# Keeping B's product operands in DRAM and splitting two of seven products once more in a two-level Strassen matmul with GELU

Groups, products and steps are counted from one in the prose, as in the prediction (the code counts from zero).

## Chip, cores, metric

One core of one Trainium2 chip. The metric is the device time of one launch in microseconds, measured as the median of several runs of the same kernel. Runs before the change agree within 0.2%. All runs in this document are fast: none took over 1.5% longer than the fastest run of its kernel.

## The reference

```python
a, b: float32 [4096, 4096], standard normal
x = np.matmul(a, b)
out = 0.5 * x * (1 + np.tanh(np.sqrt(2 / np.pi) * (x + 0.044715 * x**3)))   # float32
```

## The kernel before

A and B are cast to fp16 while they are loaded. The output is made in 16 groups, each of four 512 x 512 blocks (one from each quadrant), by seven products instead of eight. A product is 4 steps (quarters of K) of 16 matmuls of 512 columns. Two accumulators, X and Y, hold the running sums in PSUM, four banks each.

```python
PRODUCTS = [                # name, accumulator, A's operand, B's operand
    ("M3", "Y", "11", ("12", "22", 1)),
    ("M5", "X", ("11", "12", -1), "22"),
    ("M7", "X", ("12", "22", -1), ("21", "22", 1)),
    ("M1", "X", ("11", "22", -1), ("11", "22", -1)),
    ("M4", "X", "22", ("21", "11", 1)),
    ("M2", "Y", ("22", "21", -1), "11"),
    ("M6", "Y", ("21", "11", -1), ("11", "12", 1)),
]
AHEAD = 2                   # VectorE makes a step's operand sums two steps ahead
```

The operands are sums of blocks, made by VectorE (tiles `aS` and `bS`, three buffers each, so at most two steps ahead):

```python
def make_sums(gi, s, q, ...):
    ...
    nc.vector.tensor_tensor(out=x, in0=y, in1=z, op=ALU.add if o[2] > 0 else ALU.subtract)
```

B's block changes at nearly every group and is loaded again from the input. A's block changes after groups 4, 8 and 12. It comes through two staging buffers and a transpose on VectorE, whose instructions run strictly in program order:

```python
    if na:                                     # A's block changes after group gi
        at(gi, 3, 0, move_slots, a_slot, nxt_a)
    for c in range(CH):
        if na:
            at(gi, 4, c, load, (load_a, (mb1, "11", c)))          # GpSimd's queue
            at(gi, 5, 2 * c, turn_a, mb1, "11", c)                # VectorE transpose
            at(gi, 5, 2 * c + 1, load, (load_a, (mb1, "12", c)))
            at(gi, 6, 2 * c, turn_a, mb1, "12", c)
            at(gi, 6, 2 * c + 1, load, (load_a, (mb1, "22", c)))
            at(gi + 1, 0, 2 * c + 1, turn_a, mb1, "22", c)
            at(gi + 1, 1, c, load, (load_a, (mb1, "21", c)))
            at(gi + 1, 3 + c, 0, turn_a, mb1, "21", c)
```

`at(gi, s, q, ...)` puts work before step q of product s of group gi in the program. Besides, ScalarE squares every block of A and B once and VectorE adds the squares up ("energy"), for a guard against numbers that fp16 would not hold. One set of squares costs VectorE 30 additions and a "weighing" (its final summing up).

## Time and profile before

| | before |
|---|---|
| time, median (range); the profiled run | 1579.12 us (1578.19 to 1580.8); 1578.57 |
| TensorE (PE) busy | 1567.7 of 1577.1 us, 7246 matmuls |
| what PE waited for, all told | 4.2 us |
| VectorE (DVE) busy | 1233.7 us |
| bytes through DMA | 211 MB |

The lines themselves, and what they say of the bound, are in the prediction. I add one measure, worked out from the trace: the time from a group's first matmul to the next group's. Before the change it is 96.69 us in every group from the third to the fifteenth (448 matmuls x 0.2158 us). So every microsecond above that is a loss with a place.

### The profile page before, as it was taken

Reading aid. Unit: us, or ns where it says so; the run is one execution under the profiler, and the core shown is the slowest. Engines: PE = TensorE matmul, PEld = TensorE weight load, DVE = VectorE, ACT = ScalarE, POOL = GpSimd, SP = SyncE. Lnnn points to the kernel's source line nnn. Section 1 sums busy time; section 2 is a strip of 40 time slices with the busy share of each in tenths; the row PEclk is TensorE's granted clock in tenths of the full one; section 3 lists DMA queues with packets and bytes.
Section 4 is the critical chain, followed back from the end, with each engine's and each line's share of the span. In section 5 each row is a group of like instructions: output and inputs, shape, how many; then the busy total and the mean of one; then the engine's idle time right before and its main releaser. Section 6 shows DMA issues by size and latency. Waiting matters only on the chain. (4 is left out here: it accounts for less than half of the span.)

```text
span 1577.1 us, 19678 instructions
## 1 busy us (share of the span) xinstructions
PE 1567.7 (99%) x7246; PEld 709.6 (45%) x7246; DVE 1233.7 (78%) x1381; ACT 518.0 (33%) x710; POOL 537.7 (34%) x980
## 2 busy tenths in 40 slices
PE   9999999999999999999999999999999999999998
PEld 4444444444444444444444444444444444444443
DVE  1698888967787888895778778887687778988775
ACT  1036445311122545531111344542211145364111
POOL 7753442420234144341124413245011443314400
PEclk9999999999999999999999999999999999999999
DMA  9999884882968378686597937679468885747802
GB/s 173 198 215 189 132 162 79 161 162 48 193 106 158 87 131 160 108 179 115 87 161 117 186 72 142 146 113 182 79 121 146 134 160 93 151 105 134 161 28 82
DMA packets 225047, 211.13 MB, mean 134 GB/s; under 512 B 20144, under 2 KB 192176, under 8 KB 224944
## 3 DMA queue, kind: packets, MB, share of 16 engines
q0 software_dynamic: 187648, 142.67, 61.7%
q1 hardware_dynamic: 37296, 67.13, 11.8%
q8 instruction: 59, 0.97, 0.2%
q14 instruction: 44, 0.36, 0.1%
HBM read 285.22 MB, written 67.11 MB: 223 GB/s over the span
## 5 line engine op out<-in xcount | busy, mean ns | idle before, releaser
L331 PEld LDWEIGHTS <-aS 128*128 128x128 f16 x4960 | 485.3, 98 | 587.2 <-issue 2.2
L186 POOL DMA_DIRECT2D bR<-in_b_dram x832 | 447.6, 544 | 700.0 <-DVE bS L302 329.7
L302 DVE TENSOR_TENSOR aS<-aT 128x2048 f16<-128x2048 f16 (+1 forms) x312 | 376.1, 1212 | 151.0 <-PE accX L331 114.5
L331 PE MATMUL accX<-bS,aS 128*128 128x512 f16 x1984 | 431.1, 379 | 0.0
L302 DVE TENSOR_TENSOR bS<-bR 128x2048 f16<-128x2048 f16 x310 | 376.1, 1218 | 69.3 <-PE accX L331 58.5
L331 PEld LDWEIGHTS <-aT 128*128 128x128 f16 x1984 | 194.2, 98 | 234.8 <-issue 0.8
L422 ACT ACTIVATE y<-y 128x512 f32<-128x512 f32 x192 | 118.5, 630 | 351.8 <-DVE y L431 351.4
L331 PE MATMUL accY<-bS,aS 128*128 128x512 f16 x992 | 216.7, 379 | 1.8 <-DVE y L431 1.8
L331 PE MATMUL accY<-bS,aT 128*128 128x512 f16 x992 | 216.9, 379 | 0.5 <-DVE bS L302 0.5
L331 PE MATMUL accX<-bS,aT 128*128 128x512 f16 x992 | 216.7, 379 | 0.0
L331 PE MATMUL accX<-bR,aS 128*128 128x512 f16 x992 | 216.7, 379 | 0.0
L331 PE MATMUL accY<-bR,aS 128*128 128x512 f16 x992 | 216.7, 379 | 0.0
L186 POOL DMA_DIRECT2D stage<-in_a_dram x144 | 89.9, 630 | 249.0 <-DVE aT L161 178.0
L431 DVE TENSOR_TENSOR energy<-energy,square 128x1024 bf16<-128x1024 bf16 x240 | 164.4, 685 | 9.5 <-ACT square L207 5.7
L395 ACT COPY x<-accX 128x512 f32<-128x512 f32 x128 | 74.9, 585 | 224.3 <-PE accX L331 224.3
L207 ACT ACTIVATE square<-aT 128x1024 bf16<-128x1024 f16 x120 | 123.4, 1051 | 70.6 <-DVE energy L431 70.2
L207 ACT ACTIVATE square<-bR 128x1024 bf16<-128x1024 f16 x120 | 123.0, 1050 | 62.5 <-DVE energy L431 60.5
L161 DVE STREAM_TRANSPOSE aT<-stage 128x2048 uint32<-128x2048 uint32 (+1 forms) x37 | 74.6, 2017 | 46.0 <-DMA stage<-in_a_dram 39.9
L395 ACT COPY m<-accX 128x512 f32<-128x512 f32 x60 | 34.7, 579 | 215.7 <-PE accX L331 213.6
L422 ACT ACTIVATE y<-accX 128x512 f32<-128x512 f32 x64 | 38.2, 597 | 100.1 <-PE accX L331 99.9
L431 DVE TENSOR_TENSOR x<-accX,x 128x512 f32<-128x512 f32 x64 | 44.0, 691 | 21.8 <-ACT y L422 19.1
L431 DVE TENSOR_TENSOR y<-accY,m 128x512 f32<-128x512 f32 x60 | 39.9, 687 | 12.5 <-ACT m L395 12.4
(38 smaller groups left out, 344.9 us busy)
## 6 DMA issues: line engine op xcount, KB each, us to landing
bR<-in_b_dram POOLq DMA_DIRECT2D x832, 128.0 KB, 5.2
out_dram<-y SPq DMA_DIRECT2D x256, 256.0 KB, 5.7
stage<-in_a_dram POOLq DMA_DIRECT2D x112, 256.0 KB, 6.8
stage<-in_a_dram POOLq DMA_DIRECT2D x32, 128.0 KB, 5.1
row<-seen_d SPq DMA_DIRECT2D x2, 1.5 KB, 4.2
seen_d<-seen SPq DMA_DIRECT2D x1, 3.0 KB, 7.4
```

Source lines behind the costliest of these rows:

```text
L161: nc.vector.transpose(dst[:, :, x, :], src[:, :, x, :])
L186: nc.gpsimd.dma_start(out=dst, in_=src)
L207: nc.scalar.activation(t[:, :], src, ACT.Square)
L302: nc.vector.tensor_tensor(out=x, in0=y, in1=z, op=ALU.add if o[2] > 0 else ALU.subtract)
L331: nc.tensor.matmul(acc[:, :], sa[:, j // 2, i * P : (i + 1) * P, j % 2], sb[:, j, :], start=start and j == 0, stop=stop and j == 3, skip_g ...
L395: nc.scalar.copy(out=t[:, :], in_=src[:, :])
L422: nc.scalar.activation(y[:, :], src[:, :], ACT.Gelu_apprx_tanh)
L431: nc.vector.tensor_tensor(out=o[:, :], in0=x[:, :], in1=y[:, :], op=op)
```

## The change

The intent is to compute less. In six groups M3 and M5 (each 512 x 2048 x 512) are themselves computed with seven products of quarters instead of eight, an eighth fewer columns. That needs more operand sums, and VectorE, busy for 1233.7 of 1577.1 us, has little room for those. So from the seventh group on B's operands are no longer made again. In the last of the first six groups that uses a block of B (groups 2, 3, 5 and 6) its sums and its plain blocks are written to DRAM. From the seventh group on they are read back ("fetched"), 1 MB at a time, into the eight buffers that held B (the ring). The operands of the split are made once per block of B, in groups 7, 8, 10 and 11 ("makers"). Groups 9 and 12 to 16 split: between the quarter products VectorE and ScalarE combine partial results ("joins").

```diff
+SPLIT = {                       # place in PSUM, A's quarters, B's quarters
+    "1": ("11", ("11", "22", -1), ("11", "22", -1)),
+    "3": ("12", "11", ("12", "22", 1)),
+    "2": ("21", ("21", "22", -1), "11"),
+    "5": ("12", ("12", "11", -1), "22"),
+    "4": ("21", "22", ("21", "11", 1)),
+    "7": ("11", ("12", "22", -1), ("21", "22", 1)),
+    "6": ("22", ("21", "11", -1), ("11", "12", 1)),
+}
+PAIR = [(s, p) for ps in ("213", "45", "76") for s in (0, 1) for p in ps]
+SPLIT_AHEAD = 6
+FETCH_AHEAD = 12
 ...
+    def keep_operand(key, x, src):              # written when made
+        ...
+        nc.sync.dma_start(out=dst, in_=src)
 ...
+    def multiply_split(gi, s, p):
+        ...
+            for j in range(NJ):
+                wide = p == "2" and j == 0
+                nc.tensor.matmul(
+                    banks[chain, i][:, :] if wide else out,
+                    sa[:, j // 2, r * P : (r + 1) * P, j % 2],
+                    sb[:, : NC] if wide else sb[:, j * NC // 2 : (j + 1) * NC // 2],
+                    start=p in "12" and j == 0, stop=j == NJ - 1, skip_group_check=True,
+                )
+        ...
+            if p == "2":
+                nc.scalar.copy(out=join("2"), in_=region(chain, "21", r))
+            elif p == "3":
+                joined(join("2"), region(chain, "12", r), join("2"), ALU.subtract)
+                joined(join("2"), region(chain, "11", r), join("2"), ALU.add)
+            elif p == "4":
+                nc.scalar.copy(out=region(chain, "22", r), in_=join("2"))
+                joined(join("4"), region(chain, "21", r), join("2"), ALU.add)
+            elif p == "5":
+                joined(region(chain, "11", r), join("4"), region(chain, "12", r), ALU.subtract)
 ...
-        na, nbb = mb1 != mb, nb1 != nb
+        na, nbb = mb1 != mb, nb1 != nb and gi + 1 < N_RAW        # N_RAW = 6
 ...
+    plans = [("b", gi) for gi in last_raw.values()]              # squares of B: groups 2, 3, 5, 6
+    plans += [("a", mb * NNB + (2 if mb else 3)) for mb in range(NMB)]   # of A: 4, 7, 11, 15
 ...
+    def fetch(key, x):
+        t = split_tiles[key] = ring_tile(x, "bK")
+        nc.gpsimd.dma_start(out=t, in_=kept_unit(*key[1:])[:, :])
 ...
+        ready = position[gi - 1, NP - 1, 3] if groups[gi][0] != groups[gi - 1][0] else 0
```

(The bookkeeping of the ring and of the steps is cut.) Two things matter for what follows. The fetches go into the same in-order queue of GpSimd as A's loads, and each waits there until its ring buffer is free. And A's loads and transposes stay where they were in the program.

More of the change, by code (lines that the diff above doesn't have):

```diff
@@ L279, in product, with kept_unit, keep_raw @@
         return (LAST if gi == len(groups) - 1 else PRODUCTS)[s]
+    kept = {}
+    def kept_unit(*key):
+        if key not in kept:
+            name = "k" + "_".join(str(x) for x in key)
+            kept[key] = dram_pool.tile([P, 2 * 4 * NC], F16, name=name, tag=name)
+        return kept[key]
+    def keep_operand(key, x, src):
+        dst = kept_unit(*key)[:, x * 4 * NC : (x + 1) * 4 * NC]
+        if len(src.shape) == 3:
+            dst = dst.rearrange("p (x y) -> p x y", x=src.shape[1])
+        nc.sync.dma_start(out=dst, in_=src)
+    def keep_raw(nb, name, quad, c):
+        nc.sync.dma_start(
+            out=kept_unit(nb, name, c)[:, :], in_=b_tiles[nb, quad, c].rearrange("p x y -> p (x y)")
+        )
     def make_sums(gi, s, q, only=None, h=None):
         mb, nb = groups[gi]
-        _, _, oa, ob = product(gi, s)
+        name, _, oa, ob = product(gi, s)
         got = []
@@ L305, in make_sums @@
             got.append(t)
+            if tag == "bS" and gi == last_raw[nb]:
+                keep_operand((nb, name, q // 2), q % 2, t[:, :])
             if tag == only:
@@ L315, in half_path @@
         order = order[-1:] + order[:-1]
+    N_RAW = NNB + 2
+    last_raw = {nb: max(g for g in range(N_RAW) if groups[g][1] == nb) for nb in range(NNB)}
+    maker = {nb: min(g for g in range(N_RAW, len(groups)) if groups[g][1] == nb) for nb in range(NNB)}
     banks = {}
@@ L391, in multiply, with region, join, joined @@
                 settle(gi, name, i)
+    joins = {}
+    def region(chain, hw, r):
+        h, w = int(hw[0]) - 1, int(hw[1]) - 1
+        return banks[chain, h * RT // 2 + r][:, w * NC // 2 : (w + 1) * NC // 2]
+    def multiply_split(gi, s, p):
+        name, chain = product(gi, s)[:2]
+        place = SPLIT[p][0]
+        sa, sb = sums.pop((gi, s, p))
+        sa = sa.rearrange("p jj (m e) -> p jj m e", e=2)
+        h = int(place[0]) - 1
+        for r in range(RT // 2):
+            i = h * RT // 2 + r
+            if p in "12":
+                bank(gi, chain, i)
+            out = region(chain, place, r)
+            for j in range(NJ):
[5 more added lines that the diff above has]
+                    start=p in "12" and j == 0, stop=j == NJ - 1, skip_group_check=True,
+                )
+            if p in "76":
+                settle(gi, name, i)
+        if p in "24":
+            joins[chain, p] = pool.tile([P, NC], F32, name="join", tag="x1", bufs=RT)
+        for r in range(RT // 2):
+            def join(p):
+                return joins[chain, p][:, r * NC // 2 : (r + 1) * NC // 2]
+            def joined(out, x, y, op):
+                nc.vector.tensor_tensor(out=out, in0=x, in1=y, op=op)
+            if p == "2":
[8 more added lines that the diff above has]
+                joined(region(chain, "11", r), join("4"), region(chain, "12", r), ALU.subtract)
     def keep(tag, src, bufs):
@@ L473, in half_path @@
     steps += [(0, s, q) for s in range(NP) for q in range(QPH // 2, QPH)]
-    steps += [(gi, s, q) for gi in range(1, len(groups)) for s in range(NP) for q in range(QPH)]
+    for gi in range(1, len(groups)):
+        if gi >= N_RAW and gi != maker[groups[gi][1]]:
+            steps += [(gi, s, p) for s, p in PAIR]
+        else:
+            steps += [(gi, s, q) for s in (0, 1) for q in range(QPH)]
+        steps += [(gi, s, q) for s in range(2, NP) for q in range(QPH)]
     position = {step: n for n, step in enumerate(steps)}
+    first_step = {gi: min(n for step, n in position.items() if step[0] == gi) for gi in range(len(groups))}
     before = {}
@@ L480, in at @@
             q = max(q, QPH // 2)
-        before.setdefault(position[gi, s, q], []).append((fn, args))
+        n = position.get((gi, s, q))
+        if n is None:
+            n = first_step[gi] + s * len(SPLIT) + 2 * q
+        before.setdefault(n, []).append((fn, args))
     for n, whats in (
@@ L546, in half_path @@
                 at(gi, 6, 2 * c + 1, load, (load_b, (nb1, "11", c)))
-    for mb in range(NMB):
-        for which, gi in (("b", mb * NNB + 1), ("a", mb * NNB + 2)):
-            blk = groups[gi][which == "b"]
-            pieces = [
-                (quad, c, h) for quad in ("22", "12", "21", "11")
-                for c in range(CH) for h in range(NJ // 2)
-            ]
-            n_two = len(pieces) - NP * QPH + 2
-            for x, piece in enumerate(pieces):
-                n = max(x // 2, x - n_two)
-                at(gi, n // QPH, n % QPH, square, which, blk, *piece)
-                at(gi, (n + 1) // QPH, (n + 1) % QPH, add_squares)
-            at(gi, 6, 2, weigh, which)
+    for nb, gi in last_raw.items():
+        for s, (name, _, _, ob) in enumerate(PRODUCTS):
+            for c in range(CH) if isinstance(ob, str) else ():
+                at(gi, s, 2 * c, keep_raw, nb, name, ob, c)
+    plans = [("b", gi) for gi in last_raw.values()]
+    plans += [("a", mb * NNB + (2 if mb else 3)) for mb in range(NMB)]
+    for which, gi in plans:
+        blk = groups[gi][which == "b"]
+        pieces = [
+            (quad, c, h) for quad in ("22", "12", "21", "11")
+            for c in range(CH) for h in range(NJ // 2)
+        ]
+        n_two = len(pieces) - NP * QPH + 2
+        for x, piece in enumerate(pieces):
+            n = max(x // 2, x - n_two)
+            at(gi, n // QPH, n % QPH, square, which, blk, *piece)
+            at(gi, (n + 1) // QPH, (n + 1) % QPH, add_squares)
+        at(gi, 6, 2, weigh, which)
     said = {}
@@ L578, in half_path, with task @@
     at(len(groups) - 1, 4, 0, read)
+    free = {}
+    for tag in ("aS", "bS"):
+        free[tag] = [position[N_RAW - 1, NP - 1, q] for q in range(QPH - AHEAD - 1, QPH)]
+    ring = [("22", 0), ("22", 1), ("21", 0), ("21", 1), ("12", 0), ("11", 0), ("12", 1), ("11", 1)]
+    ring_end = {x: position[N_RAW - 1, s, q] for x, (s, q) in enumerate(
+        [(3, 1), (3, 1), (4, 1), (4, 1), (6, 0), (6, 0), (6, 1), (6, 1)]
+    )}
+    n_ring = 0
+    tasks = {}
+    split_tiles = {}
+    def task(n, fn, *args):
+        tasks.setdefault(n, []).append((fn, args))
@@ new lines, in ring_place, with ring_tile @@
+    def ring_place(need, ahead):
+        nonlocal n_ring
+        x = n_ring % len(ring)
+        n_ring += 1
+        n = max(ring_end[x] + 1, need - ahead)
+        assert n <= need, (steps[need], steps[n])
+        return x, n
+    def ring_tile(x, name):
+        quad, c = ring[x]
+        t = pool.tile([P, NJ, NC], F16, name=name, tag=f"bR{b_slot0[quad]}{c}")
+        return t.rearrange("p x y -> p (x y)")
+    def fetch(key, x):
+        t = split_tiles[key] = ring_tile(x, "bK")
+        nc.gpsimd.dma_start(out=t, in_=kept_unit(*key[1:])[:, :])
@@ new lines, in take, with quarter_a, quarter_b, blocks_a @@
+    def take(t, op, y, z):
+        nc.vector.tensor_tensor(out=t, in0=y, in1=z, op=ALU.add if op > 0 else ALU.subtract)
+    def quarter_a(tiles, hk):
+        h, k = int(hk[0]) - 1, int(hk[1]) - 1
+        return tiles[k][:, :, h * TM : (h + 1) * TM]
+    def quarter_b(tiles, kw):
+        k, w = int(kw[0]) - 1, int(kw[1]) - 1
+        return tiles[k].rearrange("p (x y) -> p x y", x=NJ)[:, :, w * NC // 2 : (w + 1) * NC // 2]
+    def blocks_a(gi, o):
+        if isinstance(o, str):
+            return [a_tiles[groups[gi][0], o, c] for c in range(CH)]
+        return [
+            split_tiles["d", gi, c].rearrange("p (jj m) -> p jj m", jj=NJ // 2) for c in range(CH)
+        ]
@@ new lines, in open_block, with block_sum, operand_a @@
+    def open_block(gi, c, x):
+        split_tiles["d", gi, c] = ring_tile(x, "aD")
+    def block_sum(gi, o, q):
+        w = 4 * NC
+        t = split_tiles["d", gi, q // 2][:, (q % 2) * w : (q % 2 + 1) * w]
+        mb = groups[gi][0]
+        take(t, o[2], part(a_tiles, mb, o[0], q), part(a_tiles, mb, o[1], q))
+    def operand_a(gi, s, q, tag):
+        o = product(gi, s)[2]
+        t = pool.tile([P, 4 * NC], F16, name="aS", tag=tag, bufs=AHEAD + 1)
+        if q in SPLIT:
+            y, z, op = SPLIT[q][1]
+            blocks = blocks_a(gi, o)
+            t = t.rearrange("p (jj m) -> p jj m", jj=NJ // 2)
+            take(t[:, :, :], op, quarter_a(blocks, y), quarter_a(blocks, z))
+        else:
+            mb = groups[gi][0]
+            take(t[:, :], o[2], part(a_tiles, mb, o[0], q), part(a_tiles, mb, o[1], q))
+        sums["a", gi, s, q] = t
@@ new lines, in operands @@
+    def operands(gi, s, q):
+        name, _, oa, _ = product(gi, s)
+        sa = sums.pop(("a", gi, s, q), None)
+        w = 4 * NC
+        nb = groups[gi][1]
+        if q in SPLIT:
+            if sa is None:
+                sa = quarter_a(blocks_a(gi, oa), SPLIT[q][1])
+            k = PAIR.index((s, q))
+            sb = split_tiles[gi, nb, "split", k // 2][:, (k % 2) * w : (k % 2 + 1) * w]
+        else:
+            if sa is None:
+                sa = part(a_tiles, groups[gi][0], oa, q)
+            sb = split_tiles[gi, nb, name, q // 2][:, (q % 2) * w : (q % 2 + 1) * w]
+        sums[gi, s, q] = sa, sb
@@ new lines, in make_split @@
+    def make_split(gi, s, p):
+        nb = groups[gi][1]
+        blocks = [split_tiles[gi, nb, product(gi, s)[0], c] for c in range(CH)]
+        o = SPLIT[p][2]
+        if isinstance(o, str):
+            t = quarter_b(blocks, o)
+        else:
+            t = pool.tile([P, 4 * NC], F16, name="bS", tag="bS", bufs=AHEAD + 1)
+            take(
+                t.rearrange("p (x y) -> p x y", x=NJ)[:, :, :],
+                o[2], quarter_b(blocks, o[0]), quarter_b(blocks, o[1]),
+            )
+            t = t[:, :]
+        k = PAIR.index((s, p))
+        keep_operand((nb, "split", k // 2), k % 2, t)
@@ new lines, in half_path @@
+    b_slot0 = dict(b_slot)
+    for gi in range(len(groups) - 1):
+        if groups[gi + 1][1] != groups[gi][1] and gi + 1 < N_RAW:
+            b_slot0 = {quad: b_slot0[nxt_b[quad]] for quad in b_slot0}
+    n_a = 0
+    last_a = 0
+    for gi in range(N_RAW, len(groups)):
+        n0, nb = first_step[gi], groups[gi][1]
+        split = (gi, 0, "1") in position
+        made = gi == maker[nb]
+        mine = [n for n in range(n0, first_step.get(gi + 1, len(steps)))]
+        ready = position[gi - 1, NP - 1, 3] if groups[gi][0] != groups[gi - 1][0] else 0
+        units, block_users = {}, []
+        makes = [
+            (position[gi, s + 1 + k // QPH, k % QPH], s, p)
+            for s in (0, 1) for k, p in enumerate("1346725")
+        ] if made else []
+        for n in mine:
+            _, s, q = steps[n]
+            name, _, oa, ob = product(gi, s)
+            block = q in SPLIT and not isinstance(oa, str)
+            if block and q == PAIR[0][1]:
+                places = [ring_place(n, SPLIT_AHEAD) for c in range(CH)]
+                e = max(ready, last_a, *(e for _, e in places))
+                for c, (x, _) in enumerate(places):
+                    task(e, open_block, gi, c, x)
+                for qq in range(QPH):
+                    task(e, block_sum, gi, oa, qq)
+                last_a = e
+            o = SPLIT[q][1] if q in SPLIT else oa
+            e = n
+            if not isinstance(o, str):
+                tag = "aS" if made or n_a % 2 else "bS"
+                n_a += 1
+                e = max(n - (SPLIT_AHEAD if q in SPLIT else AHEAD), ready, last_a, free[tag][-AHEAD - 1] + 1)
+                assert e <= n, steps[n]
+                free[tag].append(n)
+                last_a = e
+                task(e, operand_a, gi, s, q, tag)
+            if block:
+                block_users.append(max(e, n if isinstance(o, str) else 0))
+                for x, _ in places:
+                    ring_end[x] = max(block_users)
+            task(n, operands, gi, s, q)
+            key = (gi, nb, "split", PAIR.index((s, q)) // 2) if q in SPLIT else (gi, nb, name, q // 2)
+            if key not in units:
+                units[key], e = ring_place(n, FETCH_AHEAD)
+                task(e, fetch, key, units[key])
+            ring_end[units[key]] = max(n, *(e for e, s1, _ in makes if s1 == s)) if s < 2 and made else n
+        for e, s, p in makes:
+            task(e, make_split, gi, s, p)
+            if not isinstance(SPLIT[p][2], str):
+                free["bS"].append(e)
@@ L589, in half_path @@
                 gi, s, q = steps[n + AHEAD]
-                if s >= 0:
+                if s >= 0 and gi < N_RAW:
                     make_sums(gi, s, q)
+            for fn, args in tasks.get(n, ()):
+                fn(*args)
             if step[:2] != (0, 2):
@@ L596, in half_path @@
                 plain(n)
+            elif step[2] in SPLIT:
+                multiply_split(*step)
             else:
```

## The prediction

> **What bounds the kernel now.** I read the page's first block, then the groups, then TensorE's own waits, then the timeline inside one step, and last the table of windows. The chain that ended last holds only the final GELU (0% of the span), so it carries nothing.
>
> ```profile
> span 1577.1 us, 19678 instructions
> ...
> PE 1567.7 (99%) x7246; PEld 709.6 (45%) x7246; DVE 1233.7 (78%) x1381; ACT 518.0 (33%) x710; POOL 537.7 (34%) x980
> ...
> PEclk9999999999999999999999999999999999999999
> ...
> q0 software_dynamic: 187648, 142.67, 61.7%
> q1 hardware_dynamic: 37296, 67.13, 11.8%
> ...
> L331 PEld LDWEIGHTS <-aS 128*128 128x128 f16 x4960 | 485.3, 98 | 587.2 <-issue 2.2
> L302 DVE TENSOR_TENSOR bS<-bR 128x2048 f16<-128x2048 f16 x310 | 376.1, 1218 | 69.3 <-PE accX L331 58.5
> ```
>
> PE is busy 99%, but its ends are modelled, so that alone proves little. Its waits prove it: this is all that it waited for in the whole run.
>
> ```profile
> PE accY L331 <- DVE y L431: 1.8, 1, 1.8
> PE accX L343 <- DVE table L583: 1.4, 1, 1.4
> PE accY L331 <- DVE bS L302: 0.5, 1, 0.5
> PE accY L362 <- DMA bR<-in_b_dram: 0.5, 1, 0.5
> ```
>
> 4.2 us of 1577. So the time is the number of matmuls times their spacing. The timeline of one step of 16 matmuls gives it:
>
> ```profile
> 799.68 3.62 PE L331 MATMUL accY<-bS,aT 128*128 128x512 f16 x16
> 800.12 2.90 PEld L331 LDWEIGHTS <-aT 128*128 128x128 f16 x14
> ```
>
> The stretch ends with a 0.379 us latency, so the spacing is (3.62 - 0.38) / 15 = 0.216 us. 7246 times that is 1565 us. A matmul takes its time from its 512 columns, and a weight load (98 ns) hides inside it. Only fewer columns can make this kernel faster, and only if nothing new makes PE wait.
>
> Room beside PE is not the same everywhere. Windows around the change of A's block between the eighth and ninth group (the boundary is near 796 us):
>
> ```profile
> 766.00:780.00 14.00, 14.00 (x66) 6.37 (x65) 11.51 (x11) 2.39 (x4) 3.44 (x6) 1.00 0.56 119
> 780.00:794.00 14.00, 14.00 (x66) 6.35 (x65) 13.93 (x13) 2.42 (x4) 4.19 (x7) 1.00 1.32 218
> 794.00:808.00 14.00, 14.00 (x67) 6.35 (x65) 11.88 (x12) 2.37 (x4) 5.09 (x8) 1.00 1.24 209
> 808.00:822.00 14.00, 14.00 (x67) 6.36 (x65) 7.30 (x6) 0.00 (x0) 2.55 (x4) 1.00 0.98 131
> ```
> ```profile
> 807.16 2.31 DVE L161 STREAM_TRANSPOSE aT<-stage 128x2048 uint32<-128x2048 uint32 x1 [2.12 <-DMA stage<-in_a_dram]
> ```
>
> The columns are PE, PEld, DVE, ACT, POOL, clock, DMA share, GB/s. VectorE is full (13.93 of 14 us) and the DMA engines are full (share 1.32; packets overlap, so 1 is not the ceiling) for about 40 us, and a transpose already waits 2.12 us for its load. Everywhere else there is room.
>
> **What the Trainium skill says.** "TensorE: Matmul & The Clock Gate", section "Back-to-back issue gap": N/2.4 + 2.5 ns, so 215.8 for 512 columns and 109.2 for 256. The trace agrees at 512 (216); no 256-column matmul runs before. "VectorE: DVE Perf Modes", section "The TRN2 errata": an fp32 tensor_tensor takes (N+151)/0.96 ns, 691 for 512. The trace has 680 to 691, so a 256-column join should take about 424. "DMA: Bandwidth & Descriptors", section "Measured (HBM→SBUF, 128 partitions, SWDGE, issued from GpSimd)": 1 MB in 6.15 us alone, 425 GB/s for large transfers. In the full windows above, A's loads write 512-byte halves of what they read, so some 180 GB/s written beside the outputs is 360 read: near that ceiling. "PSUM — Partial Sum Buffer", section "The four PSUM rules": the first flag clears a whole bank, later groups in it start without the flag, and engine writes leave the bits alone. That explains why product 2 opens its bank with one full-width matmul: region 22 must have its bits set before ScalarE seeds it. No run here shows this yet.
>
> **The change, part by part.**
>
> TensorE. Six groups (9, 12 to 16) split M3 and M5. Each was 64 matmuls of 512 columns: 64 x 0.216 = 13.8 us. Now seven products of 2 x 8 = 16 matmuls are 112, of which 110 have 256 columns and 2 the full width: 110 x 0.1092 + 2 x 0.216 = 12.4 us. A split thus saves 1.4 us, twelve of them 16.5 us (an eighth of twelve times 13.8 would be 20.7; the 2.5 ns per matmul and the wide ones eat 4). This lies wholly on the bounding engine. New count of matmuls: 7246 + 12 x 48 = 7822.
>
> VectorE, steady state. From the seventh group on, 20 B sums of 1.22 us a group go away (24 us). Four groups (7, 8, 10, 11) instead make ten split B sums once (12 us). A split group adds 5 A sums for M3, and 4 block sums and 1 more for M5 (12 us), and 16 joins of some 0.42 us (7 us). So VectorE falls by 5 us in a split group and by 12 in a maker. None of that shortens the run, since VectorE does not bound it.
>
> VectorE, placement. B's squares move into groups 2, 3, 5, 6, and A's first set into group 4. Groups 4 and 5 then hold squares and transposes: 40 sums x 1.22 + 32 accumulates and weighing 26 + 4 transposes x 2.3 + 24 other operations x 0.69 = 100 us by durations. VectorE overlaps successive operations a little (a sum every 1.13 us), and the same sum for group 2 gives 91 where the window shows 85.9, so 95 of the 96.7 us that PE takes. It just fits, with products in which it lags.
>
> DMA. B's raw loads fall from 13 blocks to 5 of 8.4 MB. Added: 14.7 MB written per block, four times, 7.3 MB of split operands, four times, and 14.7 to 17.8 MB read back in each of ten groups: some 88 MB written, 166 MB read. Written with 4 to 8 KB rows this is about 36 us of all engines per 14.7 MB at the ceiling, against 97 us per group. It is hidden, except where A's block changes too.
>
> **Rivals.**
>
> (1) The saving arrives whole: 1578.6 - 16.5 = 1562. For: PE waits 4 us now, fetches go out up to 12 steps ahead, VectorE's mean load falls.
>
> (2) The two changes of A's block that precede a split group (8 to 9 and 12 to 13) take part of it back. There VectorE may not begin the new block's sums before the old group's last step, and gets eight at once. From the third step before the boundary to M3's seventh product it must do 15 sums x 1.13, 3 transposes x 2.23, 4 settling operations x 0.62 and 12 joins x 0.40 = 31 us, while PE needs 3 x 3.45 + 10 x 1.75 + 0.4 = 28.3. That is 2.7 us short even if no load is late. And A's loads (5.7 us each at 360 GB/s) now share one queue with megabyte fetches (2.6 us each), in stretches that were already full: the last transposes may find their data 3 to 8 us later, and the joins queue behind them in order. I take 3.5 us of PE waiting for each, up to 9. Groups 12, 15 and 16, with squares or weighing next to the split, are short by about a microsecond each by the same sum. With that: 1562 + 7 + 3 = 1572.
>
> (3) A weight load becomes the bound. It takes 98 ns against 109 of a 256-column matmul, 11 ns of slack. If the pair needed 120, a split would take 13.6 us and the gain would be 3 us: 1576 before any wait, and 1586 with the waits of (2). Against: loads start with the preceding matmul in the timeline, so 98 fits.
>
> (4) The writes to DRAM hold the B sums' three buffers, or the early groups run out of DMA (group 5: 8.4 MB raw, 14.7 MB kept, half of A). Then PE would wait in groups 2 to 6, 5 to 15 us: 1577 to 1587. Against: a sum is held three steps (10 us) by PE anyway, and an output of 256 KB landed in 5.7 us.
>
> **Range and chances.** The saving is well founded, since it is a count times a spacing. The losses are a tally of queues, and I took the low half of it because an ordering with leads this particular looks tuned. Predicted: 1572 us; 8 times in 10 between 1560 and 1586. More than 2% faster would need 1547, below the 1562 that the arithmetic allows, so 0.02. More than 2% slower needs 1610, three rivals at their worst at once: 0.04. Within 2%: 0.94.
>
> **What would show it.** Right: 1320 matmuls of 256 columns spaced 0.109 us; M3 plus M5 of group 13 or 14 in about 25 us instead of 27.6; some 10 us in PE's waits, gathered at the start of groups 9 and 13 (counting from one) and put down to VectorE's joins, sums or transposes; DMA bytes near 400 MB. Rival 1 is right if PE's waits stay under 5 us. Rival 3 if the spacing is well above 0.109 with no wait shown. Rival 4 if PE waits in groups 2 to 6, on B sums behind writes. My prediction is wrong if PE's waits pass 25 us, or if the split steps run slower than their columns.

## The result, and the profile after

| | before | after |
|---|---|---|
| time, median (range), same rounds | 1579.12 us (1578.19 to 1580.8) | 1623.1 us (1613.88 to 1629.42) |
| profiled run, span | 1577.1 us | 1627.9 us |
| ratio, 95% interval | | 1.0273 (1.0212 to 1.0333) |

The change made the kernel 2.7% slower; I had predicted 1572 us, within 1560 to 1586. A ratio here is the mean time of one kernel's fast runs over that of the other's of the same rounds, so it is not quite the ratio of the medians. The changed kernel also scatters by 1%, where the one before scatters by 0.2%. The changed kernel's profiled run is the slowest of the four (1629.42 us), so the losses read from it below are some 6 us above those of a median run.

The page of the changed kernel:

```profile
span 1627.9 us, 20781 instructions
...
PE 1570.3 (96%) x7822; PEld 771.2 (47%) x7822; DVE 1153.2 (71%) x1377; ACT 535.6 (33%) x758; POOL 349.0 (21%) x626
...
PE   9999999999999999999878999999998799999998
...
PEclk9999999999999999999999999999999899999999
...
q0 software_dynamic: 136672, 241.21, 60.2%
q1 hardware_dynamic: 73520, 155.22, 25.7%
```

The 576 more matmuls are as counted, and since 1320 of them have 256 columns, PE streams 1.2% fewer columns than before; yet the span grew. The row of tenths shows two dents in PE, in slices 20 to 22 and 31 to 32 (40.7 us each, counted from one: 773 to 895 and 1221 to 1302 us). VectorE's total fell by 80 us. Totals do not show the cause; PE's waits do (who waited, for whom, us in total, times, longest):

```profile
PE accX L374 <- DMA bK<-k_M: 16.2, 2, 10.3
PE accX L456 <- DVE y L522: 9.1, 4, 4.3
PE accY L374 <- DVE bS L338: 6.2, 2, 3.9
PE accY L456 <- DVE aS L721: 6.0, 2, 4.8
PE accY L374 <- DVE aS L721: 5.2, 1, 5.2
PE accY L374 <- DVE y L522: 4.0, 3, 1.8
PE accY L456 <- DVE accY L471: 3.6, 3, 1.7
```

Few waits, each long: on sums (`aS`, `bS`), on settled outputs (`y`), on joins (`accY L471`) and twice on a fetched operand (`bK`). The times of the groups say where (from first matmul to first matmul, us; the last group to the start of its last matmul plus one spacing; groups without a row are at 96.69, or at 93.95 where split, but for the first, which took 119.2 us before and 118.6 after):

| group | before | after | after, without any wait | loss |
|---|---|---|---|---|
| 2 | 97.4 | 100.8 | 97.4 | 3.4 |
| 4, 5 | 96.7, 96.7 | 102.7, 98.3 | 96.7, 96.7 | 7.6 |
| 8, 9 | 96.7, 96.7 | 110.5, 110.8 | 96.7, 93.95 | 30.6 |
| 12, 13 | 96.7, 96.7 | 96.8, 114.0 | 93.95, 93.95 | 22.9 |
| 15, 16 | 96.7, 96.7 | 95.6, 95.3 | 93.95, 93.95 | 3.0 |

The sum closes: six split groups save 6 x 2.74 = 16.4 us, the losses are 67.5, the first group is 0.6 shorter, and 67.5 - 16.4 - 0.6 = 50.5 us, against a span that grew by 50.8. So 53.5 us were lost in the four groups around the two later changes of A's block.

Part of a loss is not waiting. After a long wait TensorE runs at half its clock for some microseconds. Counted from the starts in the trace of the changed kernel, 51 matmuls of 512 columns are spaced some 427 ns instead of 216, and 50 of 256 columns 213 instead of 109: together 15.8 us beyond their normal spacing. Before the change there are none after the warm-up. The timeline of PE shows one such place, in M7 of group 9; the columns are start, length, engine, line, operation, count, and in brackets the idle time before and what ended it:

```profile
855.13 7.07 PE L374 MATMUL accX<-bK,aS 128*128 128x512 f16 x32
868.05 17.12 PE L374 MATMUL accX<-bK,aS 128*128 128x512 f16 x65 [5.85 <-DMA bK<-k_M]
```

65 matmuls take 17.1 us, or 16.7 without the last one's latency of 0.38: 0.261 us each instead of 0.216. The extra 2.9 us are the cold clock. The trace's own record of the clock has 0.5 there for 6.8 us. The Trainium skill states the mechanism ("TensorE: Matmul & The Clock Gate", section "Part 1: The HAM clock gate"): half clock after an idle window of some 3.4 us, full clock after a busy one. This trace agrees on the halving, but shows it already after a gap of 2.6 us between two starts.

Now the place itself. First GpSimd's queue around the first load of A's new block, before the change and then after (idle before in brackets):

```profile
712.70 5.27 POOL L186 DMA_DIRECT2D stage<-in_a_dram  x8 [1.07 <-DMA bR<-in_b_dram]
774.63 1.91 POOL L186 DMA_DIRECT2D stage<-in_a_dram  x3 [56.66 <-DVE aT L161]
```
```profile
753.08 0.54 POOL L718 DMA_DIRECT2D bK<-k_M  x1 [40.21 <-DVE bS L721]
...
772.10 0.54 POOL L718 DMA_DIRECT2D bK<-k_M  x1 [14.65 <-DVE aS L721]
...
774.13 1.97 POOL L202 DMA_DIRECT2D stage<-in_a_dram  x3
```

Before, the first two loads (eight transfers) went out at 712.7 us, some 60 us ahead of their transposes, because GpSimd had nothing else to wait for. After, the same queue stands for 40 and then 15 us in front of fetches whose ring buffers are not free, and the first load goes out at 774.1. Then the loads themselves are slow. Time from issue to landing (least, median, most) of A's loads, before, 774 to 812 us, and after, 774 to 849 us:

```profile
DMA to landing us min/median/max: 4.3/6.4/10.0
```
```profile
DMA to landing us min/median/max: 8.8/14.0/17.4
```

And VectorE, in its order, waits for each, with the old group's sums standing behind the transposes:

```profile
789.78 2.31 DVE L177 STREAM_TRANSPOSE aT<-stage 128x2048 uint32<-128x2048 uint32 x1 [7.26 <-DMA stage<-in_a_dram]
792.01 2.32 DVE L721 TENSOR_TENSOR aS<-aT 128x2048 f16<-128x2048 f16 x2
798.39 2.31 DVE L177 STREAM_TRANSPOSE aT<-stage 128x2048 uint32<-128x2048 uint32 x1 [4.06 <-DMA stage<-in_a_dram]
...
818.86 2.31 DVE L177 STREAM_TRANSPOSE aT<-stage 128x2048 uint32<-128x2048 uint32 x1 [7.56 <-DMA stage<-in_a_dram]
821.10 2.32 DVE L721 TENSOR_TENSOR aS<-aT 128x2048 f16<-128x2048 f16 x2
```

PE waited 5.2 us for the sums at 792.0 and 4.8 us for those at 821.1. In the second case that is the split's first operand. In the first it is a sum of the old block, for M2, which needs nothing of the new one: it only stands behind the transpose.

### The profile page after: what moved, and what is told of

Its sections match the earlier page's. It is cut to its first block, busy times and chain, and to the rows that moved or that the text cites. A ratio compares the mean times of both kernels' runs of the same rounds, so it can differ in the third digit from the quotient of the medians.

```text
span 1627.9 us, 20781 instructions
## 1 busy us (share of the span) xinstructions
PE 1570.3 (96%) x7822; PEld 771.2 (47%) x7822; DVE 1153.2 (71%) x1377; ACT 535.6 (33%) x758; POOL 349.0 (21%) x626
## 2 busy tenths in 40 slices
DMA packets 210299, 397.83 MB, mean 244 GB/s; under 512 B 16912, under 2 KB 139792, under 8 KB 187920
## 5 line engine op out<-in xcount | busy, mean ns | idle before, releaser
L374 PE MATMUL accX<-bK,aS 128*128 128x512 f16 x1536 | 338.1, 382 | 16.2 <-DMA bK<-k_M 16.2
L374 PE MATMUL accY<-bK,aS 128*128 128x512 f16 x1280 | 281.0, 382 | 5.7 <-DVE aS L721 5.2
L721 DVE TENSOR_TENSOR aS<-aT 128x2048 f16<-128x2048 f16 x206 | 244.7, 1216 | 54.6 <-PE accX L374 40.4
L513 ACT ACTIVATE y<-y 128x512 f32<-128x512 f32 x192 | 119.2, 629 | 386.1 <-DVE y L522 386.0
L202 POOL DMA_DIRECT2D bR<-in_b_dram x320 | 172.9, 544 | 231.0 <-DMA bR<-in_b_dram 98.8
L718 POOL DMA_DIRECT2D bK<-k_M x116 | 62.4, 540 | 604.8 <-DVE aS L721 125.2
L374 PE MATMUL accX<-bS,aS 128*128 128x512 f16 x704 | 153.1, 379 | 0.1
L338 DVE TENSOR_TENSOR aS<-aT 128x2048 f16<-128x2048 f16 (+1 forms) x112 | 134.1, 1200 | 23.7 <-PE accX L374 15.9
L338 DVE TENSOR_TENSOR bS<-bR 128x2048 f16<-128x2048 f16 x110 | 133.4, 1217 | 16.7 <-PE accX L374 16.5
L374 PE MATMUL accX<-bK,aT 128*128 128x512 f16 x640 | 139.8, 379 | 0.0
L177 DVE STREAM_TRANSPOSE aT<-stage 128x2048 uint32<-128x2048 uint32 (+1 forms) x37 | 74.6, 2017 | 67.5 <-DMA stage<-in_a_dram 59.8
L374 PE MATMUL accY<-bS,aT 128*128 128x512 f16 x352 | 80.4, 390 | 6.2 <-DVE bS L338 6.2
## 6 DMA issues: line engine op xcount, KB each, us to landing
stage<-in_a_dram POOLq DMA_DIRECT2D x112, 256.0 KB, 10.3
k_M<-bR SPq DMA_DIRECT2D x16, 1024.0 KB, 12.2
```

The lines of the kernel that those rows point to most:

```text
L177: nc.vector.transpose(dst[:, :, x, :], src[:, :, x, :])
L202: nc.gpsimd.dma_start(out=dst, in_=src)
L374: nc.tensor.matmul(acc[:, :], sa[:, j // 2, i * P : (i + 1) * P, j % 2], sb[:, j, :], start=start and j == 0, stop=stop and j == 3, skip_g ...
L513: nc.scalar.activation(y[:, :], src[:, :], ACT.Gelu_apprx_tanh)
L718: nc.gpsimd.dma_start(out=t, in_=kept_unit(*key[1:])[:, :])
L721: nc.vector.tensor_tensor(out=t, in0=y, in1=z, op=ALU.add if op > 0 else ALU.subtract)
```

## The experiments

Theory: A's loads and the fetches get into each other's way at the two later changes of A's block, in one queue and on the same DMA engines; late transposes then hold VectorE, and VectorE holds PE. Main rivals: the split steps and their bursts of sums cost the time by themselves; or there are simply too many bytes. Every experiment gave the right result except where noted. They were run in four batches, each beside the kernel before, so runs of different batches are best compared by their ratios.

| run | median us | ratio to before, 95% interval | loss in groups 8, 9, 12, 13 | loss in 4, 5 |
|---|---|---|---|---|
| changed kernel | 1623.1 | 1.0273 (1.0212 to 1.0333) | 53.5 | 7.6 |
| A not reloaded | 1576.8 | 0.9984 (0.9968 to 1.0001) | 1.5 | 7.4 |
| fetches on SP | 1608.78 | 1.0195 (1.0178 to 1.0212) | 31.9 | 8.7 |
| no split | 1600.03 | 1.0130 (1.0113 to 1.0147) | 13.4 | 8.2 |
| A's first loads earlier | 1603.22 | 1.0144 (1.0107 to 1.0181) | 34.9 | 4.8 |
| A spread | 1584.68 | 1.0042 (1.0016 to 1.0068) | 7.6 | 8.5 |
| A spread, fetches on SP | 1608.16 | 1.0187 (1.0170 to 1.0204) | 31.7 | 8.0 |
| A spread, squares moved | 1581.79 | 1.0014 (0.9996 to 1.0032) | 4.4 | 9.9 |
| squares moved only | 1624.09 | 1.0286 (1.0240 to 1.0333) | 45.2 | 12.2 |
| all spread | 1574.28 | 0.9963 (0.9950 to 0.9977) | 7.6 | 3.0 |
| all spread, copies first | 1600.56 | 1.0143 (1.0126 to 1.0159) | 8.2 | 3.0 |
| copies first only | 1650.84 | 1.0482 (1.0443 to 1.0521) | 47.9 | 7.8 |

Losses are in us, from the profiled run of each, as in the table above.

### A's block not reloaded (wrong result)

```diff
+        if na and mb:
+            before.setdefault(first_step[gi + 1] - 4, []).append((same_a, (mb, mb1)))   # reuse A's old tiles
+        na = na and not mb
```

> A's block is not reloaded at the two changes that precede a split group (wrong result for half of the rows, on purpose): their loads and transposes are gone, the split steps, the fetches and the burst of eight sums stay. Theory 1 (A's loads and the fetches collide there: TensorE lost 31 us in groups 8 and 9 and 23 us in 12 and 13 of the changed kernel's trace): those losses fall below 3 us each and the time to about 1572 us. Rival (the split steps or the burst of sums themselves cost the time): the losses stay and the time is above 1600 us.

The time fell to 1576.8 us. Windows of exactly one group each, group 8 and then group 9 with its split (columns: window, length, PE, PEld, DVE, ACT, POOL, clock, DMA share, GB/s):

```profile
711.70:808.40 96.70, 96.70 (x449) 43.83 (x448) 56.70 (x59) 15.28 (x26) 6.44 (x12) 1.00 0.70 250
808.40:902.40 94.00, 94.00 (x546) 53.28 (x545) 50.58 (x67) 20.55 (x38) 10.25 (x19) 1.00 0.70 258
```

PE is busy for the whole of both. Groups 8, 9 and 13 lost nothing, with the fetches, the split, its joins and the burst of eight sums all in place. So the split steps do what they were meant to: 96.69 becomes 93.95, 2.74 us a group. The rival that the split costs the time by itself falls. The run takes away A's loads, their transposes and VectorE's time for them together, so it does not tell which of these does the harm. The time came out 5 us above the expected 1572; groups 2, 4, 5, 12, 15 and 16, which were not touched, still lost 15.5 us together.

### Fetches on the SP queue

```diff
-        nc.gpsimd.dma_start(out=t, in_=kept_unit(*key[1:])[:, :])
+        nc.sync.dma_start(out=t, in_=kept_unit(*key[1:])[:, :])
```

> The fetches of kept operands are issued from the SP queue, so that A's loads no longer stand behind fetches that wait for a ring slot. Theory 1a (the order of one queue delays A's loads): A's first load goes out some 50 us before its transpose, as before the change, and the time falls to 1575 to 1590 us. Rival 1b (the DMA engines simply have too much to move in these 60 us): the loads still land in about 14 us and the time stays at 1605 to 1630 us. It can also turn out that outputs now wait behind fetches on SP, and VectorE on their buffers.

14 us came back, less than theory 1a asked for; the time lies in rival 1b's range. A's loads were now free of the fetches' waits (the first two went out from 544 us on, over 230 us ahead of their transposes), but those that followed landed later than ever. Their landing times in this run, 784 to 865 us:

```profile
DMA to landing us min/median/max: 5.1/18.9/39.1
```

So VectorE waited for A's loads longer than without this edit: 33.1 us against 18.9 between 700 and 910 us, and 29.6 against 10.4 between 1110 and 1330. What came back is the other half of the collision: TensorE no longer waited for a fetch in M7, which had been 16.2 us in two waits. The order in one queue is thus only a part of it. The engines are shared whatever queue issues: the Trainium skill says so ("DMA: Bandwidth & Descriptors", section "Issuing engines are not separate DMA queues"), and this run agrees: between 740 and 880 us the fetches landed earlier (10.3 us in the median against 16.1) and A's loads later (18.9 against 14.0).

### No split

```diff
-        if gi >= N_RAW and gi != maker[groups[gi][1]]:
+        if False:
```

and no split operands made.

> B's operands are kept and read back, but no product is split: 7246 matmuls as before. Theory 1: the collision with A's loads is there without the split, so the time is above that of the kernel before, 1590 to 1610 us. Rival (the split's joins and bursts make the loss): 1578 to 1586 us, with the 4/5 boundary's 8 us as the only loss.

With the product count of before, keeping and fetching alone cost 1.3%: groups 9 and 13 lose 7.6 and 5.8 us, and groups 4 and 5 8.2. So the collision exists without the split. The split makes it four times worse (53.5 against 13.4 us). By the program, the makers and split steps bring more writes and fetches, and the sums of the split ask for A's new block right at the boundary; how much each of these adds was not measured.

### A's first loads earlier

```diff
-                at(gi, 4, c, load, (load_a, (mb1, "11", c)))
-                at(gi, 5, 2 * c, turn_a, mb1, "11", c)
+                at(gi, 2, c, load, (load_a, (mb1, "11", c)))
+                at(gi, 4, 2 * c, turn_a, mb1, "11", c)
   ... the second quadrant's, and the third's loads, a half to one product earlier
```

> A's first loads are emitted two products earlier and its first three transposes one half to one product earlier; all else as changed. Theory 1: the waits for late transposes before the boundary go (the 5 us and 5 us on sums), those after it stay in part: 1595 to 1610 us. If only the bandwidth counts, the backlog moves but stays: above 1615 us.

1603 us, as the theory said. The waits moved: PE waited 19.8 us for two fetched operands of M7 instead of for sums. Two of A's loads were still issued inside the split, in front of those fetches.

### A's chain spread

```diff
+                    at(gi, 2, c, load, (load_a, (mb1, "11", c)))
+                    at(gi, 3, 1 + 2 * c, turn_a, mb1, "11", c)
+                    at(gi, 3 + c, 2 - 2 * c, load, (load_a, (mb1, "12", c)))
+                    at(gi, 5, 2 + c, turn_a, mb1, "12", c)
+                    at(gi, 5 + c, 3 - 2 * c, load, (load_a, (mb1, "22", c)))
+                    at(gi + 1, 0, 4 + c, turn_a, mb1, "22", c)
+                    at(gi + 1, 1, 1 + c, load, (load_a, (mb1, "21", c)))
-        ready = position[gi - 1, NP - 1, 3] if ...
+        ready = position[gi - 1, NP - 1, 1] if ...
```

> Same bytes, same queue, same split. At the two later changes of A's block each load is emitted two to five steps or more earlier against its transpose, the transposes of its third quadrant come late in the split, and the burst of sums may begin two steps earlier. If the loss is one of timing (loads that land in 14 instead of 6 us, and transposes that hold VectorE's order), groups 8, 9 and 13 lose under 10 us together instead of 51, and the time is 1575 to 1588 us. If the engines of the DMA cannot move the bytes in time, the loss stays over 25 us: above 1600 us.

> The run before this one, with the fetches on the SP queue besides. If the one queue's order still matters after the spreading, it is faster than the former by 3 us or more; if outputs stand behind fetches, slower.

The first of these is the run that weighs most (the spreading is at the two later changes only). The bytes and the queue are the same. A's loads are emitted longer before their transposes, but for the last quadrant's; the transposes themselves move away from the crowded end of the group; and the new block's sums may begin two steps earlier (`ready`). The loss fell from 53.5 to 7.6 us. The loads that went out from 760 us on land no faster than in the changed kernel:

```profile
DMA to landing us min/median/max: 5.6/14.3/18.3
```

VectorE still waits for them. Between 760 and 870 us, in the changed kernel and then in this run:

```profile
DVE aT L177 <- DMA stage<-in_a_dram: 18.9, 3, 7.6
```
```profile
DVE aT L177 <- DMA stage<-in_a_dram: 10.3, 2, 8.0
```

Around the second of these changes (1110 to 1330 us) it even waits longer, 23.5 us against 10.4, and yet group 13 lost 2.1 us instead of 20.0. So neither the number of bytes nor the length of VectorE's waits makes the loss. What is gone is TensorE's side: of its 11.2 us of waits for A's sums nothing is left (one of 1.9 us for a transpose came instead), and of the 16.2 us for fetches 2.9. So it seems to matter what stands behind the waits in the order of the engines. Which of the three moves did most was not separated. With the fetches on SP besides, it got worse again (1608 us): PE waited 13.8 us for sums behind late transposes and 8.4 us for a fetch. So with the loads spread, one queue in program order did better here than two. Why, beyond the shared engines, was not studied.

### Squares moved

```diff
+            if which == "a" and gi == NNB - 1:          # group 4: two squares to a step, done before the transposes
+                n = x // 2
+            if which == "a" and gi == len(groups) - 2:  # group 15: after its split
+                n = 8 + x // 2
```

with the weighings moved accordingly.

> Only the moves of the squares, A's loads as changed. Groups 4 and 5 lose under 2 us instead of 7.6, the changes of A's block lose what they lost: about 1612 us, and not under 1605.

> The first of these runs, with A's first squares done two to a step in the first four products of group 4, those of group 15 begun after the split, and the weighing of group 11's moved behind the next split. Theory: groups 4 and 5 lose 7.6 us because VectorE is full with squares and transposes in the last two products of group 4, so 5 to 7 us of that and some 3 us in groups 12, 15, 16 come back: 8 to 10 us faster than the first of these runs, 1566 to 1578 us.

The part for groups 12, 15 and 16 worked: in the second of these runs they lose 0.6, 0 and 0.8 us. The part for groups 4 and 5 missed: 12.2 and 9.9 us lost instead of some 2. So both times missed too: alone, the move gained nothing (1624 us against the expected 1612), and on top of the spreading 3 us instead of 8 to 10. The waits came earlier in group 4, among them 2.9 us for ScalarE (`x`), which had to square two pieces a step. The reason to suspect VectorE there is the windows of 15 us, before and then after (columns as above):

```profile
400.00:415.00 15.00, 15.00 (x71) 6.79 (x70) 15.00 (x14) 2.38 (x4) 5.09 (x8) 1.00 1.26 207
415.00:430.00 15.00, 15.00 (x72) 6.80 (x70) 8.96 (x7) 0.00 (x0) 5.08 (x8) 1.00 1.30 215
```
```profile
400.00:415.00 15.00, 13.21 (x62) 5.89 (x61) 14.96 (x16) 4.35 (x6) 3.19 (x6) 1.00 1.15 194
415.00:430.00 15.00, 11.06 (x45) 4.57 (x44) 14.76 (x18) 6.89 (x9) 4.59 (x8) 0.89 1.06 251
```

VectorE is full in both kernels up to 415 us; before, it then has 6 us to recover, after, it has none, and PE loses 1.8 and 3.9 us in these windows.

### All spread

A's chain is spread at the first change too, and the squares of group 15 move behind its split, as in the run before. Each weighing of groups 4 to 6 goes past the end of its group, where there is less to do:

```diff
+            if NNB <= gi <= N_RAW:
+                n = max(1 + x // 2, x - n_two + 1)
+        n_weigh = {3: (4, 0, 0), 4: (5, 0, 0), 5: (6, 0, 0), 6: (6, 6, 3), 10: (11, 2, 0), 14: (14, 6, 1)}
```

> As the run with A's loads spread, with A's chain spread at the first change too (its first two transposes a product and a half earlier than the crowded end of group 4), each weighing of groups 4 to 6 put after the end of its group instead of into its crowded last product, the squares of group 15 after its split, and the third and ninth group's last A loads behind a fetch that is needed sooner. By a tally of VectorE's work step by step its lag at the end of group 4 falls from 10 us to 5, which TensorE tolerates: the 7.6 us of groups 4 and 5 become under 2, those of 12, 15 and 16 under 1.5 together, those at the later changes of A stay near 5. Time 1568 to 1573 us: faster than both kernels, if only by 0.5%.

1574.28 us in five rounds, faster than both kernels: 0.37% below the one before (interval 0.23 to 0.50%). That is a gain clear of the noise, but a small one, under the 2% from which a run here is called faster. Groups 4 and 5 lose 3.0 us, group 8 6.9, groups 9, 13, 14, 15 nothing, 12 and 16 0.7 and 0.8. It missed the expected 1568 to 1573 us by 1.3 us, which is less than group 8 loses.

### The order of a maker's writes

In that trace GpSimd stood 17.3 us in front of fetches that waited for the writes of the two plain copies among the seven split operands. These leave from the ring buffers themselves, in rows of 512 bytes, while the sums leave from `bS` in rows of 4 KB. In the median the same size takes three times as long to land (KB each, median us from issue to landing, in the changed kernel's trace):

```profile
k_split<-bS SPq DMA_DIRECT2D x40, 512.0 KB, 3.7
...
k_split<-bK SPq DMA_DIRECT2D x16, 512.0 KB, 10.6
```

The median hides two kinds. In each maker the two copies of M3's block landed 4.5 to 6.3 us after their issue and the two of M5's 15.0 to 16.3 us. The last sums' writes before those took up to 10.8 us as well, against 2.6 for most of the early ones. So how much of the difference is due to the short rows, and how much to what else is under way, is not shown.

```diff
-            for s in (0, 1) for k, p in enumerate("1346725")
+            for s in (0, 1) for k, p in enumerate("2513467")
```

> The former best, with the two plain copies among a maker's seven split operands written out first instead of last. In the former's trace the fetches that reuse their ring slots waited 17 us in GpSimd's queue for those writes, and group 8 lost 7 us. If that wait is its cause, group 8 loses under 3 us and the time is 1568 to 1571 us; if the loads of A alone are, it stays at 1573 to 1575 us.

> The changed kernel with this order alone. If the writes of the copies were a main cause of its loss too, group 8 loses under 5 us instead of 14 and the time falls by 8 us or more, to 1615 us or less; group 13, which no maker precedes, keeps its 20 us. If not: within its spread, 1614 to 1630 us.

Both missed, badly: 26 us slower in one, some 28 us in the other. Group 8 did not gain, and all four makers lost 7 to 9 us each in the first of the two. Two waits of that run show why, the second being PE's largest:

```profile
DVE bS L736 <- DMA k_split<-bS: 43.2, 6, 11.4
```
```profile
PE accX L374 <- DVE aS L736: 21.8, 5, 6.5
```

The sums' writes that are issued just behind a copy now land as late as it does: in group 7 a copy issued at 645.2 us took 17.5 us, and the sums' writes at 647.6 and 648.8 us took 16.3 and 16.4. Until then they hold `bS` buffers, of which there are three; VectorE waits for a buffer, and A's sums wait behind it in VectorE's order. Before this edit that wait came to 0.2 us in the whole run. The order that the change came with had avoided this, at the price of some waiting on GpSimd. Whether a different treatment of the copies would recover group 8 was not tried.

## Why the prediction was wrong

**Saving on TensorE, 16.5 us: right.** 7822 matmuls, 256 columns spaced 109 ns, and 93.95 instead of 96.69 us in every undisturbed split group, in the run without A's reload and in the spread ones. 6 x 2.74 = 16.4. M3 plus M5 of group 14 took 24.9 us where I had named 25.

**Rival 3, weight loads as the bound: wrong.** Same figures. (Its gain of 3 us comes out as 2 from its own numbers: 12 x (13.8 - 13.63).)

**DMA bytes near 400 MB, VectorE's total lower: right** (397.83 MB; 1233.7 to 1153.2 us). Neither total said anything about the time.

**The term that failed: "I take 3.5 us of PE waiting for each, up to 9", for the two later changes of A's block.** The place was right, the size was wrong by a factor of six to nine: 30.6 us in groups 8 and 9, and 22.9 in 12 and 13, of which 1.5 are group 12's own (squares and weighing). TensorE's waits came to 51.7 us in all, past the 25 that I had named as the sign of being wrong. What the runs showed in its place:

1. I reckoned with the loads landing some 3 to 8 us later, but from the old issue times. They had been issued some 60 us ahead; now they stand behind fetches that wait for ring buffers (40 us in one case), and go out as late as the program lets them. I did not ask what an in-order queue that had been idle would now be waiting for.
2. I looked for the damage in the split's joins and first sums. It began before: a late transpose holds the old group's sums as well, and group 8, which is not split at all, lost 13.8 us (4.9 of them the wait at its end for group 9's first operand).
3. I took the fetches' lead of 12 steps as enough. In the trace M7's second operand landed 5.9 us late in group 9 and 10.3 us late in group 13; my working had A's loads and the fetches in one queue, but I followed only the loads' lateness. I had also taken a fetch at 2.6 us; from issue to landing it took 16.1 in the median between 740 and 880 us.
4. There was no term for the clock. Waits of this length cost 15.8 us on top of themselves.

The 2.7 us that I computed for the burst of sums "even if no load is late" were not tested: the run without A's reload lost nothing in groups 9 and 13, but three transposes, 6.7 us of that tally, had gone as well.

**Rival 4, the early groups: the sign came, the mechanism did not.** Groups 2, 4 and 5 lost 11.0 us, and PE waited 6.2 us there for B's sums, as the rival had said. But in the whole run VectorE waited 0.2 us for the writes of kept sums to free a buffer. In groups 4 and 5 it was full instead, as follows; group 2 stays open.

**"It just fits", for groups 4 and 5: wrong by 7.6 us.** The total did fit (95 of 96.7 us by my tally, which counts 32 accumulates where the trace has 30). The end of group 4 did not, and "everywhere else there is room" was a misreading: between 400 and 415 us VectorE was busy for 15.00 of 15 us before the change already. In that stretch sums, transposes, squares and the weighing fall into the group's last two products, and VectorE may lag by about two steps before PE feels it. Spreading that work brought 4.6 of the 7.6 back. The remaining 3.4 us of group 2 were not studied; they began with a wait of VectorE of 4.43 us for an output buffer, against 2.71 before.

**Groups 12, 15 and 16, "about a microsecond each": nearly right.** 1.5, 1.6 and 1.4 us; group 12's remaining 1.3 belong to the change after it.

**Chances.** I gave 0.04 to slower by 2%, as "three rivals at their worst at once". They were not independent: by the runs above, late loads, held sums, late fetches and the cold clock come from one collision.

What stays open: how the 53.5 us divide between the queue's order and the sharing of the engines. The run with the fetches on SP took the order away and left 31.9 us, but changed the sharing with it. Open too is which move of the spread run did most.

## What to carry to other kernels

Where a load is issued early only because its queue happens to be idle, that lead is a hidden buffer of time: before putting anything that waits into that queue, find out from the trace how far ahead the loads in it really run. An engine's mean load says little about a change; look at the fullest two or three products, add the new work there, and compare with the lag that the buffers allow. When a wait on TensorE passes two or three microseconds, count the slow clock after it as well; and before giving a change up, try whether the same work spread over more time keeps the gain, as it did here (1574 against 1579 and 1623 us).

## What the Trainium skill lacked or had wrong

- "TensorE: Matmul & The Clock Gate": the half clock is said to follow an idle window of about 3.4 us. In the changed kernel a gap of 2.6 us between two starts of matmuls (group 2) was already followed by eight spaced 427 ns, while one of 2.2 us was not. Over all thirteen traces, after the warm-up, the shortest gap with the half clock after it was 2.4 us (no split) and the longest without it 3.25 us (A spread); every gap from 3.28 us on had it. So between some 2.4 and 3.3 us it can go either way.
- The same page, "Back-to-back issue gap", gives 109.2 ns for 256 columns by its formula, and that holds (109). But it calls the formula that of an isolated matmul and gives about 131 ns at 512 columns for a stream with weight loads. Here such a stream ran at 215.8 ns, which is what the formula gives.
- "DMA: Bandwidth & Descriptors": 1 MB is given as 6.15 us of busy time, for a transfer alone. From issue to landing the 1 MB fetches of kept operands took 9.4 us in the median here (7.2 for the split's), and between 740 and 880 us all fetches 16.1 in the median and 18.9 at most. No page says how far a load falls behind when plain and casting transfers share the engines.
- The same page gives 512 bytes as the least size for line rate. Writes of 512 KB in 512-byte rows took 10.6 us to land in the median here, those in 4 KB rows 3.7 us. This is no proof against the page, since the slow ones fell into a crowded stretch (the early ones took 4.5 to 6.3 us), but no page gives the time of such writes on this chip.
- "PSUM — Partial Sum Buffer" calls 0 the only seed value that is safe either way. It has no example of the other case that its rule allows: here ScalarE and VectorE write other seeds into regions whose bits a matmul had set, and the result was correct in the nine experiments that split and were meant to be.
